# Recurrence gates of a two-block transformer: sigmoid in fp32 replaced by tanh of half the argument in three fp32r passes

## The chip, the cores and the metric

One core of one Trainium2 chip runs the whole program. The metric is the device time of one execution in microseconds (us). The engines that matter here are PE (TensorE: matrix products), DVE (VectorE) and ACT (ScalarE, which evaluates functions such as tanh, exp and the square root from a table that has to be loaded first). Each engine works through its own queue in order and waits at an instruction until what that instruction needs is there.

## The reference, cut to what matters

The reference runs two transformer blocks on 512 tokens of width 1024 in float32. The first block has a token mixer and a mixture of experts and is not touched. The second block prepends 16 meta tokens (528 rows), projects them, and combines for each of 8 heads an attention output with a recurrence over the tokens. The change lies in that recurrence, which runs once forward and once backward over each block of 128 channels:

```python
def rg_lru(xc, wa, ba, wx, bx, lam, reverse):
    ...
    r = jax.nn.sigmoid(jnp.einsum('btnc,ncd->btnd', xb, wa) + ba)
    i = jax.nn.sigmoid(jnp.einsum('btnc,ncd->btnd', xb, wx) + bx)
    log_a = RG_C * r * jax.nn.log_sigmoid(lam)
    a = jnp.exp(log_a)
    u = jnp.sqrt(-jnp.expm1(2.0 * log_a)) * (i * xf)
    _, h = lax.associative_scan(_linear_recurrence_combine, (a, u), axis=1, reverse=reverse)
```

Here `xc` is the projected input after a convolution over four tokens, `xb` the same in blocks of 128 channels, `xf` the same in float32. The output of both directions is multiplied by a gelu branch and a sigmoid gate and added to the gated attention output.

## The kernel before, in words

A matrix product that has to be nearly exact in float32 is done in three passes: both operands are split into a high part in fp32r (ACT copies it, `Net.split`, whose ACT copy is recorded at L90 and whose DVE subtraction at L170) and the low rest, and `mm3` (L196 to L200) multiplies high by high, high by low and low by high. `by_turns` reads the moving operand in two alternating halves, and `unturned` or an equivalent rearrangement puts the columns back where PSUM is read.

The stretch that the change touches is the loop in `block2` over the 8 heads n, called rounds here. PE's order is written out by hand. One round issues on PE, in this order: a projection of 24 matmuls of 512 columns (`gates`, first step), the product of the attention weights of head n-1 with the values (`attention`, L198 to L200 into psB), the gate products of the recurrence of head n (`rnn_gates`, L2046), two blocks of attention scores of head n (L198 to L200 into psD, 12 matmuls of 264 columns), the second projection, transposes of the normalized scores (L2140 with 16 rows, L2145 with 128), the third projection, two more blocks of scores, the recurrence's input projection for head n+1 (`rnn_x`, 48 matmuls of 264 columns) and again transposes. DVE and ACT are ordered by a planner which takes instructions in the order of the program as far as it expects them to be ready, so their order is not to be read from the source. Functions that need a table keep the program's order among themselves (`Net.act`).

`rnn_gates` makes four groups of products, two directions times the two gates r and i. Each group is two fp32 matmuls of 264 columns, which are recorded as two each, and fills one PSUM tile of the tag psD. There are two such tiles, shared with the attention scores and the 16-row transposes. ACT reads a group into `rg` or `ig` with a sigmoid (L90, rg<-psD and ig<-psD). They are named rg1, ig1, rg2 and ig2 below, in program order. DVE then multiplies ig by the convolved input (L2049).

In the round after, `rnn` (L2078) takes rg of head n-1: ACT makes a tanh and an exp of it and the square of that, DVE combines them (L2092). Later in the round ACT takes the two square roots, and DVE multiplies (L2098), scans (L2101), adds both directions (L2103) and multiplies by the gelu branch (L2104). The output of `attention` of head n-2 is completed behind this: an addition on DVE (L2163, ao), a split into `ga` by ACT (L90, ga<-ao) and `rn` by DVE. `rnn_x` makes the convolution in four DVE instructions (L2026, L2028).

ACT's table is loaded by an ACT_TABLE_LOAD which the compiler puts ahead of an activation that needs another one. A round has three: for the sigmoid, for the exp of the attention scores, for the square roots. Tanh needs none beside exp or sigmoid. Behind the loop the output projection follows (`mix_out`), with one square root for each of four token tiles and a gain `n2g` that a DMA brings.

Of the kernel before, what the change touches and what calls it, by code (L numbers as in the profile page):

```python
# [9 lines left out]
FT = mybir.dt.float32  # L10
FR = mybir.dt.float32r
I32 = mybir.dt.int32
BF = mybir.dt.bfloat16
AF = mybir.ActivationFunctionType
OP = mybir.AluOpType
# [38 lines left out]
def halves(x):  # L54

    return x.rearrange("p (s c) -> p s c", s=2)


def by_turns(x):

    return x.rearrange("p (s c) -> p c s", s=2)


def unturned(x):

    return x.rearrange("p (c s) -> p s c", s=2)
# [9 lines left out]
class Net:  # L76
# [1912 lines left out]
    def rnn_start(self, p, vec):  # L1989

        nc = self.nc
        x = vec[:, 72:88]
        cl = p.tile([128, 2, 16], FT, name="cl")
        y = p.tile([128, 16], FT, name="cl_y")
        c = cl[:, 0, :]
        nc.vector.scalar_tensor_tensor(y, x, -1.0, x, op0=OP.mult, op1=OP.min)
        self.act(y, y, AF.Exp)
        self.log1p_unit(p, c, y, 16)
        nc.vector.tensor_scalar(y, x, 0.0, None, op0=OP.min)
        nc.vector.tensor_tensor(c, y, c, OP.subtract)  # L2000
        nc.vector.tensor_scalar(c, c, 8.0, None, op0=OP.mult)
        nc.vector.tensor_scalar(cl[:, 1, :], c, -1.0, None, op0=OP.mult)
        return cl

    def rnn_x(self, p, n, vec, xT):

        nc, I = self.nc, self.I
        T = META + S
        H = T // 2
        nhi, nlo = xT  # L2010
        wg = p.tile([128, 2, 2, 128], FT, name="wg")
        nc.sync.dma_start(wg[:, 0], I["rg_wa_2"][0, :, n].rearrange("d c e -> c d e"))
        nc.sync.dma_start(wg[:, 1], I["rg_wx_2"][0, :, n].rearrange("d c e -> c d e"))
        hi, lo = self.wchunk(I["w_in_2"][0], 0, NK, 1536 + n * 128, 128)
        xr = p.tile([128, T + 3], FT, name="xr")
        nc.vector.memset(xr[:, 0:2], 0.0)
        nc.vector.memset(xr[:, T + 2:], 0.0)
        for j in range(2):
            js = slice(j * H, (j + 1) * H)
            ps = self.psA.tile([128, 512], FT, name="psA")  # L2020
            for k in range(NK):
                self.mm3(ps[:, :H], hi[:, k, :], lo[:, k, :], by_turns(nhi[:, k, js]), by_turns(nlo[:, k, js]),
                         k == 0, k == NK - 1)
            self.act(halves(xr[:, 2 + j * H:2 + (j + 1) * H]), unturned(ps[:, :H]), AF.Copy)
        c = p.tile([128, T], FT, name="xc")
        nc.vector.tensor_scalar(c, xr[:, 0:T], vec[:, n:n + 1], vec[:, 32 + n:33 + n], op0=OP.mult, op1=OP.add)  # L2026
        for j in range(1, 4):
            nc.vector.scalar_tensor_tensor(c, xr[:, j:j + T], vec[:, 8 * j + n:8 * j + n + 1], c,  # L2028
                                           op0=OP.mult, op1=OP.add)
        return c, wg  # L2030

    def rnn_gates(self, p, n, vec, x, meanwhile=lambda: None):

        nc = self.nc
        T = META + S
        H = T // 2
        c, wg = x
        rg = p.tile([128, 2, T], FT, name="rg")
        ig = p.tile([128, 2, T], FT, name="ig")
        for d in range(2):  # L2040
            if d:
                meanwhile()
            for w, dst, bias in ((0, rg, 40), (1, ig, 56)):
                ps = self.psD.tile([128, 2, 512], FT, name="psD")
                for j in range(2):
                    nc.tensor.matmul(ps[:, j, :H], wg[:, w, d, :], c[:, j * H:(j + 1) * H], start=True, stop=True)  # L2046
                self.act(dst[:, d, :].rearrange("p (a b) -> p a b", a=2), ps[:, :, :H], AF.Sigmoid,
                         bias=vec[:, bias + 8 * d + n:bias + 8 * d + n + 1])
        nc.vector.tensor_tensor(ig, ig, c[:, None, :].to_broadcast([128, 2, T]), OP.mult)  # L2049
        return rg, ig  # L2050

    def gates(self, p, n, xT, rn, ga):
# [25 lines left out]
    def rnn(self, p, n, cl, st, rn):  # L2078

        nc = self.nc  # L2080
        T = META + S
        rg, ig = st
        u = p.tile([128, 2, T], FT, name="th", bufs=1)
        for d in range(2):
            q = 8 * d + n
            r, t = rg[:, d, :], u[:, d, :]
            self.act(t, r, AF.Tanh, scale=cl[:, 1, q:q + 1])
            self.act(r, r, AF.Exp, scale=cl[:, 0, q:q + 1])

            a2 = p.tile([128, T], FT, name="a2", bufs=1)  # L2090
            self.act(a2, r, AF.Square)
            nc.vector.scalar_tensor_tensor(t, a2, 1.0, t, op0=OP.add, op1=OP.mult)  # L2092
        yield
        for d in range(2):
            self.act(u[:, d, :], u[:, d, :], AF.Sqrt, scale=0.0625)
        for d in range(2):
            t, g, r = u[:, d, :], ig[:, d, :], rg[:, d, :]
            nc.vector.tensor_tensor(g, g, t, OP.mult)  # L2098
            if d:
                t, g, r = t[:, ::-1], g[:, ::-1], r[:, ::-1]  # L2100
            nc.vector.tensor_tensor_scan(t, r, g, 0.0, op0=OP.mult, op1=OP.add)  # L2101
        f = u[:, 0, META:]
        nc.vector.tensor_tensor(f, f, u[:, 1, META:], OP.add)  # L2103
        nc.vector.tensor_tensor(rn[n], rn[n], f, OP.mult)  # L2104
        yield
# [227 lines left out]
```

## Time and profile before

| | us |
|---|---|
| median of 3 runs | 1918.06 (1916.91 to 1920.73) |
| the profiled execution | 1921.64 |
| its span, first to last instruction | 1919.8 |
| PE busy in the span | 1805.8 |
| DVE busy in the span | 990.5 |
| ACT busy in the span | 709.1 |

The profiled execution's own time is 1.84 us longer than its span. The loop over the heads lies between about 1244 and 1536 us of the span, a round of it takes 34.7 us. The recorded duration of a matmul includes its latency and overlaps with the next, so what a matmul costs is read from the distance between two starts.

### The profile page before, as it was taken

The numbers are of one execution on the slowest core, as the hardware profiler recorded it, in microseconds if no ns is written. First come the engines' busy times: TensorE is split into PE (matmuls) and PEld (weight loads), VectorE is DVE, ScalarE is ACT, GpSimd is POOL, SyncE is SP. The second block draws the span as 40 slices with busy tenths as digits, with TensorE's granted clock in tenths as the row PEclk, the third lists the DMA queues.
The fourth block names the chain that finished last, engine by engine and source line by source line (L and its number), as shares of the span: only waits on it lengthen the run. The fifth ranks groups of instructions, "written<-read, shape, count | busy, mean of one in ns | idle before, by whom it ended". The sixth has DMA issues, their size and how long they took to land.

```text
span 1919.8 us, 23894 instructions
## 1 busy us (share of the span) xinstructions
PE 1805.8 (94%) x9309; PEld 1365.1 (71%) x9309; DVE 990.5 (52%) x1834; ACT 709.1 (37%) x1157; POOL 30.5 (2%) x39
## 2 busy tenths in 40 slices
PE   6999999989999899989898879999999989999999
PEld 5787888868898734434333336888888778888887
DVE  6853787745466523222121249657878863333332
ACT  5243443424323311101010126467677733322322
POOL 0000000000000000000000000000000000000000
PEclk9999999989999899999999999999999999999999
DMA  8645766876288699999999973432221233333331
GB/s 257 96 119 99 123 93 87 148 180 88 72 292 308 241 372 425 424 426 425 424 425 425 383 301 121 122 104 78 72 76 56 88 99 110 99 100 107 101 121 66
DMA packets 251988, 372.13 MB, mean 194 GB/s; under 512 B 30369, under 2 KB 192706, under 8 KB 227938
## 3 DMA queue, kind: packets, MB, share of 16 engines
q1 hardware_dynamic: 241218, 342.79, 56.3%
q10 hardware_dynamic: 7632, 16.78, 2.3%
q0 software_dynamic: 3024, 11.01, 1.5%
q8 instruction: 74, 1.21, 0.3%
q14 instruction: 40, 0.33, 0.0%
HBM read 348.51 MB, written 22.04 MB: 193 GB/s over the span
## 4 chain that ended last, share of the span: by engine, by line
PE 56%; DMA 21%; DVE 14%; ACT 7%; issue 3%; SPq 0%; POOL 0%; ACTq 0%; DVEq 0%
DMA mwt<-in_w 16%; PE psA L199 13%; PE psA L200 12%; PE psA L198 12%; PE psB L1289 4%; DVE wlo L170 2%; PE psB L1322 2%; DMA raw<-in_w_in 2%; ACT whi L90 1%; DVE th L2101 1%; PE psA L1108 1%; PE psB L603 1%; PE psB L649 1%; DVE yc L594 1%; ACT th L90 1%
## 5 line engine op out<-in xcount | busy, mean ns | idle before, releaser
L90 ACT ACTIVATE whi<-raw 128x1024 fp32r<-128x1024 f32 (+1 forms) x203 | 233.4, 1156 | 418.1 <-PE psA L199 267.6
L170 DVE TENSOR_TENSOR wlo<-raw,whi 128x1024 fp32r<-128x1024 f32 (+1 forms) x195 | 249.8, 1283 | 242.7 <-ACT whi L90 230.3
L1289 PE MATMUL psB<-mwt,XT 128*64 128x512 f32 x1008 | 236.3, 602 | 12.7 <-DMA mwt<-in_w 9.9
L1289 PEld LDWEIGHTS psB<-mwt,XT 128*64 128x64 f32 x1008 | 79.3, 138 | 157.5 <-issue 131.3
L200 PE MATMUL psA<-hT_hi,wlo 128*128 128x512 f32 (+1 forms) x456 | 176.2, 386 | 9.2 <-DVE wlo L170 9.2
L199 PE MATMUL psA<-hT_lo,whi 128*128 128x512 f32 (+1 forms) x456 | 177.3, 389 | 0.0
L198 PE MATMUL psA<-hT_hi,whi 128*128 128x512 f32 (+1 forms) x456 | 175.9, 386 | 0.9 <-ACT whi L90 0.9
L1354 DVE TENSOR_TENSOR res<-res,psA 128x512 f32<-128x512 f32 x128 | 79.4, 682 | 126.3 <-PE psA L1349 126.3
L1322 PE MATMUL psB<-mwt,hbT 128*64 128x512 f32 x480 | 118.6, 596 | 22.6 <-DMA mwt<-in_w 21.3
L199 PE MATMUL psA<-hn_lo,whi 128*128 128x512 f32 (+1 forms) x368 | 136.4, 371 | 0.3 <-DVE hn_lo L2197 0.3
L198 PE MATMUL psA<-hn_hi,whi 128*128 128x512 f32 (+1 forms) x368 | 136.5, 371 | 0.2 <-ACT hn_hi L90 0.2
L200 PE MATMUL psA<-hn_hi,wlo 128*128 128x512 f32 (+1 forms) x368 | 136.3, 370 | 0.0
L1298 DVE TENSOR_TENSOR sl<-sl,psB 128x512 f32<-128x512 f32 x16 | 11.0, 688 | 193.7 <-PE psB L1289 193.7
L198 PE MATMUL psA<-xn_hi,whi 128*128 128x512 f32 (+1 forms) x320 | 109.4, 342 | 0.4 <-ACT qx L90 0.4
L200 PE MATMUL psA<-xn_hi,wlo 128*128 128x512 f32 (+1 forms) x320 | 108.2, 338 | 0.0
L199 PE MATMUL psA<-xn_lo,whi 128*128 128x512 f32 (+1 forms) x320 | 108.1, 338 | 0.0
L1322 PEld LDWEIGHTS psB<-mwt,hbT 128*64 128x64 f32 x480 | 36.3, 136 | 98.5 <-issue 57.2
L200 PEld LDWEIGHTS psA<-hT_hi,wlo 128*128 128x128 f32 (+1 forms) x456 | 86.1, 189 | 21.8 <-DVE wlo L170 10.2
L198 PEld LDWEIGHTS psA<-hT_hi,whi 128*128 128x128 f32 (+1 forms) x456 | 86.1, 189 | 13.6 <-ACT whi L90 1.3
L90 ACT ACTIVATE XT<-psA 128x512 f32<-128x512 f32 x32 | 17.5, 594 | 211.6 <-PE psA L1266 206.2
L199 PEld LDWEIGHTS psA<-hT_lo,whi 128*128 128x128 f32 (+1 forms) x456 | 86.1, 189 | 11.9
L198 PEld LDWEIGHTS psA<-hn_hi,whi 128*128 128x128 f32 x368 | 69.6, 189 | 9.5 <-ACT hn_hi L90 0.5
(571 smaller groups left out, 3489.8 us busy)
## 6 DMA issues: line engine op xcount, KB each, us to landing
mwt<-in_w SPq DMA_DIRECT2D x188, 1024.0 KB, 20.7
raw<-in_w_in SPq DMA_DIRECT2D x108, 512.0 KB, 7.2
raw<-in_w_ffn_in SPq DMA_DIRECT2D x44, 512.0 KB, 3.9
raw<-in_w_ffn_out SPq DMA_DIRECT2D x22, 512.0 KB, 3.6
raw<-in_w_pa SPq DMA_DIRECT2D x8, 512.0 KB, 4.3
raw<-in_w_pb SPq DMA_DIRECT2D x8, 512.0 KB, 5.1
raw<-in_w_o SPq DMA_DIRECT2D x8, 512.0 KB, 4.5
raw<-in_w_out SPq DMA_DIRECT2D x8, 512.0 KB, 3.6
```

The lines of the kernel that those rows point to most:

```text
L90: ins = self.nc.scalar.activation(out, in_, func, **kw)
L170: return self.nc.vector.tensor_tensor(lo, x, hi.bitcast(FT), OP.subtract)
L198: nc.tensor.matmul(out, whi, xhi, start=first, stop=False)
L199: nc.tensor.matmul(out, whi, xlo, start=False, stop=False)
L200: nc.tensor.matmul(out, wlo, xhi, start=False, stop=last)
L594: conv = nc.vector.scalar_tensor_tensor(yc, xc[:, j:j + S], self.cw[:, 24 * j + m:24 * j + m + 1], yc, op0=OP.mult, op1=OP.add)
L603: nc.tensor.matmul(psn[:, n, m:m + 1], sq[:, n * 128:(n + 1) * 128], one, start=True, stop=True)
L649: nc.tensor.matmul(ps[:, j, :, :], qk[:, h, 0, tok], qk[:, h, :, tok], start=True, stop=True)
L1108: nc.tensor.matmul(ps[:, k, :], self.res[:, t, :].rearrange("p (f k) -> p k f", k=NK)[:, k0 + k, :], P0[:, t, :], start=(t == 0), stop=(t ...
L1289: nc.tensor.matmul(ps[CAP * i:CAP * (i + 1), :], XT[:, r0 + k, CAP * i:CAP * (i + 1)], w_, start=(r0 + k == 0), stop=(r0 + k == NK - 1))
L1322: nc.tensor.matmul(pys[half][CAP * i:CAP * (i + 1), :], hT[:, r0 + k, CAP * i:CAP * (i + 1)], ws[i][:, k, half * 512:(half + 1) * 512], st ...
L1354: nc.vector.tensor_tensor(x, x, unturned(ps), OP.add)
```

## The change

The weights of the gate products and the convolved input are split into a high and a low part and the products go through `mm3`, three fp32r passes in place of one fp32 product. The sigmoid becomes a tanh of half the argument, and what follows is adapted: sigmoid(x) is (1 + tanh(x/2))/2, so the bias and the decay constants are halved ahead of the loop, ig gets its 1 added in the DVE multiplication, and the constants of tanh, exp and square root take up the rest. Behind the two square roots a tanh of one column into a scrap tile is added. The convolved input, the high part of the weights and the low part of the input have one buffer each, the high part of the input shares the two buffers of `xr`, and the low part of the weights those of `wg`.

```diff
@@ -1998,7 +1998,9 @@
         self.log1p_unit(p, c, y, 16)
         nc.vector.tensor_scalar(y, x, 0.0, None, op0=OP.min)
         nc.vector.tensor_tensor(c, y, c, OP.subtract)
-        nc.vector.tensor_scalar(c, c, 8.0, None, op0=OP.mult)
+        nc.vector.tensor_scalar(c, c, 4.0, None, op0=OP.mult)
+
+        nc.vector.tensor_scalar(vec[:, 40:72], vec[:, 40:72], 0.5, None, op0=OP.mult)
         nc.vector.tensor_scalar(cl[:, 1, :], c, -1.0, None, op0=OP.mult)
         return cl
 
@@ -2011,6 +2013,8 @@
         wg = p.tile([128, 2, 2, 128], FT, name="wg")
         nc.sync.dma_start(wg[:, 0], I["rg_wa_2"][0, :, n].rearrange("d c e -> c d e"))
         nc.sync.dma_start(wg[:, 1], I["rg_wx_2"][0, :, n].rearrange("d c e -> c d e"))
+        ws = p.tile([128, 2, 2, 128], FR, name="wghi", bufs=1), p.tile([128, 2, 2, 128], FR, name="wg")
+        self.split(*ws, wg)
         hi, lo = self.wchunk(I["w_in_2"][0], 0, NK, 1536 + n * 128, 128)
         xr = p.tile([128, T + 3], FT, name="xr")
         nc.vector.memset(xr[:, 0:2], 0.0)
@@ -2022,19 +2026,21 @@
                 self.mm3(ps[:, :H], hi[:, k, :], lo[:, k, :], by_turns(nhi[:, k, js]), by_turns(nlo[:, k, js]),
                          k == 0, k == NK - 1)
             self.act(halves(xr[:, 2 + j * H:2 + (j + 1) * H]), unturned(ps[:, :H]), AF.Copy)
-        c = p.tile([128, T], FT, name="xc")
+        c = p.tile([128, T], FT, name="xc", bufs=1)
         nc.vector.tensor_scalar(c, xr[:, 0:T], vec[:, n:n + 1], vec[:, 32 + n:33 + n], op0=OP.mult, op1=OP.add)
         for j in range(1, 4):
             nc.vector.scalar_tensor_tensor(c, xr[:, j:j + T], vec[:, 8 * j + n:8 * j + n + 1], c,
                                            op0=OP.mult, op1=OP.add)
-        return c, wg
+        cs = p.tile([128, T + 3], FR, name="xr")[:, 0:T], p.tile([128, T], FR, name="xclo", bufs=1)
+        self.split(*cs, c)
+        return c, cs, ws
 
     def rnn_gates(self, p, n, vec, x, meanwhile=lambda: None):
 
         nc = self.nc
         T = META + S
         H = T // 2
-        c, wg = x
+        c, (chi, clo), (whi, wlo) = x
         rg = p.tile([128, 2, T], FT, name="rg")
         ig = p.tile([128, 2, T], FT, name="ig")
         for d in range(2):
@@ -2043,10 +2049,13 @@
             for w, dst, bias in ((0, rg, 40), (1, ig, 56)):
                 ps = self.psD.tile([128, 2, 512], FT, name="psD")
                 for j in range(2):
-                    nc.tensor.matmul(ps[:, j, :H], wg[:, w, d, :], c[:, j * H:(j + 1) * H], start=True, stop=True)
-                self.act(dst[:, d, :].rearrange("p (a b) -> p a b", a=2), ps[:, :, :H], AF.Sigmoid,
+                    js = slice(j * H, (j + 1) * H)
+                    self.mm3(ps[:, j, :H], whi[:, w, d, :], wlo[:, w, d, :], by_turns(chi[:, js]), by_turns(clo[:, js]),
+                             True, True)
+                self.act(dst[:, d, :].rearrange("p (a s c) -> p a s c", a=2, s=2),
+                         ps[:, :, :H].rearrange("p a (c s) -> p a s c", s=2), AF.Tanh, scale=0.5,
                          bias=vec[:, bias + 8 * d + n:bias + 8 * d + n + 1])
-        nc.vector.tensor_tensor(ig, ig, c[:, None, :].to_broadcast([128, 2, T]), OP.mult)
+        nc.vector.scalar_tensor_tensor(ig, ig, 1.0, c[:, None, :].to_broadcast([128, 2, T]), op0=OP.add, op1=OP.mult)
         return rg, ig
 
     def gates(self, p, n, xT, rn, ga):
@@ -2084,15 +2093,17 @@
         for d in range(2):
             q = 8 * d + n
             r, t = rg[:, d, :], u[:, d, :]
-            self.act(t, r, AF.Tanh, scale=cl[:, 1, q:q + 1])
-            self.act(r, r, AF.Exp, scale=cl[:, 0, q:q + 1])
+            self.act(t, r, AF.Tanh, scale=cl[:, 1, q:q + 1], bias=cl[:, 1, q:q + 1])
+            self.act(r, r, AF.Exp, scale=cl[:, 0, q:q + 1], bias=cl[:, 0, q:q + 1])
 
             a2 = p.tile([128, T], FT, name="a2", bufs=1)
             self.act(a2, r, AF.Square)
             nc.vector.scalar_tensor_tensor(t, a2, 1.0, t, op0=OP.add, op1=OP.mult)
         yield
         for d in range(2):
-            self.act(u[:, d, :], u[:, d, :], AF.Sqrt, scale=0.0625)
+            self.act(u[:, d, :], u[:, d, :], AF.Sqrt, scale=0.25 ** 3)
+
+        self.act(self.small.tile([128, 1], FT, name="warm"), cl[:, 0, 0:1], AF.Tanh)
         for d in range(2):
             t, g, r = u[:, d, :], ig[:, d, :], rg[:, d, :]
             nc.vector.tensor_tensor(g, g, t, OP.mult)
```

## Rows read from the trace of the kernel before

**Rows 1.** The page's part 1: engine, busy us, share, instructions.
```profile
PE 1805.8 (94%) x9309; PEld 1365.1 (71%) x9309; DVE 990.5 (52%) x1834; ACT 709.1 (37%) x1157; POOL 30.5 (2%) x39
```
**Rows 2.** One round as a window: length, each engine's busy us, granted clock, DMA.
```profile
1353.38:1388.07 34.69, 33.62 (x196) 29.16 (x195) 27.77 (x53) 25.53 (x45) 0.00 (x0) 1.00 0.26 77
```
**Rows 3.** PE in order of time, round 2: start us, duration us, instruction [idle before].
```profile
1318.77 3.89 PE L2046 MATMUL psD<-xc,wg 128*128 128x264 f32 x16
1323.54 0.38 PE L198 MATMUL psD<-kThi,qhi 128*128 128x264 f32 x1 [0.88 <-ACT rg L90]
...
1324.99 0.38 PE L198 MATMUL psA<-xn_hi,whi 128*128 128x512 f32 x1
...
1330.17 0.67 PE L2140 MATMUL psD<-ident,pr 128*16 128x128 f32 x2
...
1343.48 0.38 PE L2140 MATMUL psD<-ident,pr 128*16 128x128 f32 x2
...
1353.38 3.89 PE L2046 MATMUL psD<-xc,wg 128*128 128x264 f32 x16
```
**Rows 4.** PE in order of time, a run of fp32r passes: first and 34th.
```profile
1303.47 0.28 PE L198 MATMUL psA<-xn_hi,whi 128*128 128x264 f32 x1
...
1307.18 0.28 PE L198 MATMUL psA<-xn_hi,whi 128*128 128x264 f32 x1
```
**Rows 5.** ACT in order of time, round 2, around the gates.
```profile
1319.86 0.70 ACT L90 ACTIVATE rg<-psD,vec 128x528 f32<-128x528 f32 x1 [0.92 <-PE psD L2046]
...
1322.27 0.63 ACT L90 ACTIVATE ga<-ao 128x512 fp32r<-128x512 f32 x1 [0.81 <-DVE xr L2017]
1322.80 0.68 ACT L90 ACTIVATE rg<-psD,vec 128x528 f32<-128x528 f32 x1
...
1326.75 1.28 ACT L90 ACT_TABLE_LOAD   x1 [2.18 <-DVE m L2127]
1328.04 0.80 ACT L90 ACTIVATE pr<-psD,m,qs 128x528 f32<-128x528 f32 x1
```
**Rows 6.** DVE in order of time, round 2 into round 3.
```profile
1337.70 0.70 DVE L2126 TENSOR_REDUCE m<-psD 128x1 f32<-128x528 f32 x1
...
1344.54 1.33 DVE L2098 TENSOR_TENSOR ig<-ig,th 128x528 f32<-128x528 f32 x2 [0.27 <-ACT th L90]
...
1348.61 0.75 DVE L2028 SCALAR_TENSOR_TENSOR xc<-xr,vec,xc 128x528 f32<-128x528 f32 x1
...
1356.25 0.67 DVE L2163 TENSOR_TENSOR ao<-ao,rn 128x512 f32<-128x512 f32 x1
```
**Rows 7.** Groups by line and form, 1235 to 1560: count, busy us, mean ns, idle.
```profile
L90 ACT ACT_TABLE_LOAD x25 | 32.1, 1283 | 29.9 <-DVE m L2127 17.5 <-DVE th L2101 9.3 <-DVE rn L2104 3.0
...
L90 ACT ACTIVATE pr<-psD,m,qs 128x528 f32<-128x528 f32 x32 | 25.2, 789 | 4.3 <-DVE m L2127 4.2
...
L170 DVE TENSOR_TENSOR qlo<-qf,qhi 128x512 fp32r<-128x512 f32 x8 | 5.4, 677 | 1.8 <-ACT qhi L90 1.8
...
L90 ACT ACTIVATE qhi<-qf 128x512 fp32r<-128x512 f32 x8 | 5.0, 628 | 0.0
```
**Rows 8.** Who waited for whom, 1235 to 1560: us in total, times, longest.
```profile
PE psD L198 <- ACT rg L90: 5.4, 6, 1.0
...
PE psD L198 <- DVE PTlo L170: 3.0, 2, 1.8
```
**Rows 9.** Behind the last round: ACT, PE, DVE in order of time, then a window.
```profile
1528.51 1.28 ACT L90 ACT_TABLE_LOAD   x1 [2.96 <-DVE rn L2104]
1529.81 0.74 ACT L90 ACTIVATE th<-rg,cl 128x528 f32<-128x528 f32 x1
...
1544.99 0.48 PE L198 MATMUL psD<-whi,ga 128*128 128x512 f32 x1 [2.01 <-ACT ga L90]
...
1556.48 1.28 DVE L2209 SCALAR_TENSOR_TENSOR hn_tok<-hB,mo_r,n2g 128x1024 f32<-128x1024 f32 x1 [1.08 <-DMA n2g<-in_norm_g]
...
1545.00:1549.00 4.00, 4.00 (x11) 3.26 (x12) 1.89 (x2) 2.00 (x2) 0.00 (x0) 0.59 0.95 262
```

## The prediction

> **What bounds the kernel now.** I read the page's first part, which says PE [rows 1], then windows of one round, because the mean over the program hides the stage. In a round of 34.69 us PE is busy for 33.6, DVE for 27.8 and ACT for 25.5, at the full clock [rows 2]. So PE's order sets the pace of the loop, and DVE has about 7 us to spare. PE in order of time shows the two places where PE itself loses time in each of rounds 2 to 6. Scores wait 0.88 us for ACT to empty a psD tile, and a pair of small transposes takes 0.67 us where the undisturbed pair takes 0.38 [rows 3]. Both waits lead to ACT: the first to rg2, which stands behind the split of ao and so behind DVE's 0.81 us [rows 5], the second to scores whose exp waited behind a table load of 1.28 us [rows 5]. From the first gate product to the next projection PE spends 1324.99 - 1318.77 = 6.22 us, of which 3.89 are gate products [rows 3].
>
> **Gate products.** Sixteen records in 3.89 us are 0.243 each, so an fp32 product of 264 columns (two records) costs 0.486 us. Three fp32r passes cost 0.337, since 33 distances between starts make 3.71 us, 0.1124 each [rows 4]. Eight products a round: 3.89 becomes 2.70, and 1.19 us of PE work goes in each of 8 rounds, 9.5 us in all. These rows are of the same shape, reading by turns, with weights changed at each pass.
>
> **The psD handover.** Faster products meet the two psD tiles sooner. ACT starts rg1 0.12 us after the group's work (1318.77 + 4 x 0.243 = 1319.74, then 1319.86), takes 0.70, and PE follows 0.06 after the end (1322.80 + 0.68 = 1323.48, then 1323.54) [rows 3, 5]. With 0.675 a group, counted from the first product: PE ends group 2 at 1.35, ACT frees the first tile at 1.50, group 3 runs from 1.56, rg2 ends near 3.15, and the scores run from 3.2. Their 12 passes and two restarts of 0.1 put the next projection at about 4.7, if ACT takes rg2 and ig2 without anything in between. Without any handover it would be 18 + 18 = 36 passes, 4.05 us; I keep that as the other bound. So rounds 2 to 6 gain 6.22 - 4.7 = 1.5 us each, 7.6 in all. Rounds 0, 1 and 7 have no such wait or another one: there I count the 1.19 saved less a new wait of 0.4 to 0.7, and in round 7 also most of its wait of 0.7 (the six waits for rg sum to 5.4 [rows 8]): 0.5, 0.7 and 1.5. Together 10.3 us.
>
> **Table loads.** There are 25 now, three a round [rows 7]. The sigmoid's goes; the exp's moves from behind the wait for the score maxima to directly behind the roots. The first round needs one, the seven others two, the last roots one and the tanh behind them one, and the output projection's root a new one: 18. Seven fewer are 9.0 us of ACT, which is not PE's time. What counts is that exp starts 1.28 us earlier after its maximum. The transposes then find their scores, and 0.67 - 0.38 = 0.29 us goes in each round, 2.4 in all. In round 7 two blocks wait for PTlo, 3.0 us together [rows 8]; the first hangs on the same exp and I take 0.8 of its 1.2.
> A page of the Trainium skill, "ScalarE: Activation LUTs", section "What ACT_TABLE_LOAD costs", adds a drain of about 1.38 us to each load of 1.28. Here the exp follows 0.01 us after the load's end, so the trace shows no such drain; with it the seven loads would be 18.6 us of ACT.
>
> **New work on ACT and DVE.** Each round adds two ACT copies (0.63 each, as qhi), two DVE subtractions (0.68 each, as qlo) [rows 7], and a warming tanh of some 0.2 us. Second pointer operands in four activations cost at most 0.789 - 0.628 = 0.16 each by those rows, 0.6 us. ACT gains and loses about the same. DVE rises from 27.8 to 29.2 us in a round that shrinks to about 32.9: it fits, but not everywhere. From the maximum at 1337.70 to the completed ao at 1356.92 DVE has a single gap of 0.27 us [rows 6]. The split of the weights needs only a DMA and the end of the last gate products, so I place it in the gap in which DVE waits for exp, free of charge. The split of the input comes right behind the convolution, inside the closed stretch, and delays ao by 0.7 less some 0.15 that the earlier exp gives back. PE is not held by it: the convolution ends at 1349.4, one copy, one subtraction and at worst one scan of 1.2 in front end by 1352, and the gates start at 1353.38 [rows 3, 6]. If a second scan and a weight split also go ahead of it, PE waits about 0.5 us a round, 4 us in all. The halving of constants is one small DVE instruction far ahead of the loop; the DVE multiplication changes its form, not its size. Both I count at nothing.
>
> **The end.** At 1528.51 ACT waited for DVE and only then loaded exp's table [rows 9]. With the table there the chain to the last ao is 1.28 us shorter, and PE waits 2.01 us at its end. Against that, the new load ahead of the first root of the output projection is 1.28 us long, of which 1.08 lies beside the wait for n2g [rows 9], so 0.2 is lost if that DMA keeps its place and 1.28 if not. I take a net gain of 0.8. Behind PE's wait the granted clock is 0.59 for 4 us, the lower level for most of it [rows 9]; a shorter wait might save up to 1.5 us, which I leave to the range.
>
> **Sum.** 10.3 + 2.4 + 0.8 + 0.8 = 14.3 us off a span of 1919.8, whose execution took 1921.64. The median of the runs shown is 3.6 lower, so I take the difference off 1918.06 and forecast 1904. Between the bounds (no handover 4.5 more, the clock 1.5 more; a late input split 4 less, the root 1.1 less) this case reaches from 1898 to 1910.
>
> **Rivals.** First, ACT's planned order stays as it is, with the split of ao ahead of rg2. Then rounds 2 to 6 gain nothing from faster products: the next projection comes at ao + 2.76, as now, and each round changes by ao's delay less 0.29. With 0.55 of delay that is +0.3 a round, 1.3 together; the rest (about 1.3 in round 0 and 0.3 + 0.7 in round 1, 1.0 in round 7, 1.6 at the exp and the end) leaves a gain of 3.6: 1914.5. For it speaks that this is today's order in five rounds. Against it: rg2 becomes ready 0.6 us earlier and ao 0.55 later, and today rg2's products end at 1318.77 + 2.92 = 1321.69, already before the split of ao starts at 1322.27 [rows 5]. If the split goes between rg2 and ig2 instead, the gain per round is 0.2 + 0.29, near 1911.
> Second, slower: the same order, and DVE's closed stretch grows by more. The place is the convolution: the warm tanh with its load, 1.5 us, can stand ahead of the second copy to xr, which comes behind the roots today, and hold the convolution for 1.1; the weights' subtraction can fall into the stretch, 0.7. Then ao comes 0.7 + 0.7 + 1.1 - 0.15 = 2.35 later, five rounds lose 2.06 each, and with 3 us gained elsewhere the time is 1925. It decides for slower from about 2 us of ao's delay. With rg2 and ig2 ahead of the split the same delay costs little, as nobody on PE waits for ao.
> Third, the change does not do what it says with the tables: the warming tanh could bring sigmoid's table, and exp would load again behind its maximum. That leaves the PE work and the handover but not the exp: about 14.3 - 2.4 - 0.8 - 1 = 10, 1908 to 1909. Today's 25 loads are two in round 0, three in each of seven rounds and two behind the loop; so none is left for the exp that follows the tanh at 1529.81, whose load comes behind roots too [rows 7, 9]. That speaks against.
> The Trainium skill, "ScalarE activation tables: per-element evaluation and per-set limits", section "Table sets in the compiler and the runtime", says that the back end places loads by the greedy longest run, and by that rule the set that also serves the coming exps is loaded; the trace agrees at 1528.51 to 1529.81.
>
> **How the numbers follow.** Forecast 0.55; the split ahead of rg2 with a small delay, 0.18; between rg2 and ig2, 0.11; slower, 0.10; tables, 0.06. The range from 1897 to 1919 leaves out the slower case and little else. 0.2% is 3.8 us, about what a measurement can tell from no change: faster takes the forecast, the in-between and the table case, and a third of the first rival, whose centre lies just at that edge, 0.77; I give 0.03 of it to unknown collisions: 0.74. Same takes most of the first rival, 0.14; slower 0.12.
>
> **What would show it.** In the changed profile, 192 fp32r passes at 0.11 us for the gates; 18 table loads, none behind the score maxima; ACT's order rg1, ig1, rg2, ig2, then ga; rounds of about 32.9 us; next projection 4.7 us behind the first gate product. The forecast is wrong if ga still stands ahead of rg2, if PE waits at the gate products for the input's low part, or if the convolution waits for the warm tanh.

## The result and the profile after

| | before | after |
|---|---|---|
| median | 1919.93 (8 runs) | 1930.94 (8 runs, 1928.16 to 1934.38) |
| ratio to before | | 1.0053, 95% interval 1.0039 to 1.0067 |
| profiled execution, its span | 1921.64, 1919.8 | 1932.93, 1930.8 |
| rounds 0 to 6, from first gate product to first gate product | 35.72, 33.93, 34.61, 34.69, 34.69, 34.70, 31.06 | 35.73, 34.69, 35.40, 37.08, 34.70, 37.08, 32.29 |
| from the last such mark to the end of the span | 431.3 | 433.8 |

The change is slower by 11 us where 14 us faster was forecast. Of the 10.95 us between the spans the seven rounds hold 7.56 and the stretch behind them 2.5; the rest had grown ahead of the loop.

What the change does, it does. Here are groups of the changed kernel by line and form, over the loop and the output projection (1235 to 1560): count, busy us, mean ns, idle time ahead.

```profile
L90 ACT ACT_TABLE_LOAD x17 | 21.8, 1283 | 0.3
L198 PE MATMUL psD<-xr,wghi 128*128 128x264 f32 x64 | 18.9, 296 | 7.0 <-ACT rg L90 4.2 <-ACT xr L90 2.4
L170 DVE TENSOR_TENSOR xclo<-xc,xr 128x528 fp32r<-128x528 f32 x8 | 5.6, 695 | 0.7 <-ACT xr L90 0.6
L90 ACT ACTIVATE rg<-rg,cl 128x528 f32<-128x528 f32 x16 | 13.1, 820 | 0.3
L170 DVE TENSOR_TENSOR wg<-wg,wghi 128x512 fp32r<-128x512 f32 x8 | 5.5, 692 | 13.7 <-ACT wghi L90 13.7
L90 ACT ACTIVATE xr<-xc 128x528 fp32r<-128x528 f32 x8 | 5.1, 643 | 21.6 <-DVE xc L2032 21.6
```

The window holds 17 table loads in place of 25 [rows 7], and the eighteenth, which was forecast for the output projection's root, stands just behind it:

```profile
1565.54 1.28 ACT L90 ACT_TABLE_LOAD   x1
```

There are 64 times three passes, and the split instructions cost what was forecast. Rounds 2 to 4 as windows (length, busy us of PE, PEld, DVE, ACT and POOL, granted clock, DMA share and GB/s), and below them a stretch inside round 3 and one at the last gate products:

```profile
1320.45:1355.85 35.40, 33.26 (x205) 29.34 (x204) 28.59 (x54) 25.64 (x46) 0.00 (x0) 1.00 0.26 75
1355.85:1392.93 37.08, 34.93 (x205) 30.52 (x204) 30.26 (x56) 26.27 (x47) 0.00 (x0) 0.95 0.25 72
1392.93:1427.62 34.69, 33.24 (x204) 29.34 (x203) 26.89 (x52) 25.21 (x45) 0.00 (x0) 1.00 0.24 69
1388.30:1393.00 4.70, 4.70 (x14) 3.63 (x14) 4.70 (x7) 2.06 (x3) 0.00 (x0) 0.64 0.02 5
1497.00:1506.00 9.00, 8.24 (x26) 6.34 (x27) 5.25 (x7) 2.81 (x4) 0.00 (x0) 0.62 0.39 117
```

At the full clock the rounds are not shorter than before [rows 2], and two of them, with the stretch at the last gates, lose to the lower granted clock: at most 2 x 0.05 x 37.08 + 0.38 x 9.00 = 7.1 us, if PE had work all that time. The rounds themselves show less: round 3 is 1.68 longer than round 2, which has the same two waits of PE, and round 4, which lacks one of them, is 0.70 shorter than round 2, so a fall costs about 1.0 us over two rounds. Against [rows 3, 5, 6] stand ACT, DVE and PE of the changed kernel in order of time, from the roots to the scores of one round (start us, duration us, instruction, [idle before, what ended it]):

```profile
1343.63 1.28 ACT L90 ACT_TABLE_LOAD   x1
1344.92 1.18 ACT L90 ACTIVATE th<-th 128x528 f32<-128x528 f32 x2
1346.12 1.28 ACT L90 ACT_TABLE_LOAD   x1
1347.41 0.20 ACT L90 ACTIVATE warm<-cl 128x1 f32<-128x1 f32 x1
1347.52 0.37 ACT L90 ACTIVATE xr<-psA 128x264 f32<-128x264 f32 x1
...
1356.90 0.63 ACT L90 ACTIVATE ga<-ao 128x512 fp32r<-128x512 f32 x1 [2.57 <-DVE ao L2174]
1357.44 0.68 ACT L90 ACTIVATE rg<-psD,vec 128x528 f32<-128x528 f32 x1
```

```profile
1346.85 2.40 DVE L2112 TENSOR_TENSOR_SCAN th<-rg,ig 128x528 f32<-128x528 f32 x2
1349.16 0.53 DVE L2030 TENSOR_SCALAR xc<-xr,vec 128x528 f32<-128x528 f32 x1
...
1351.36 0.67 DVE L170 TENSOR_TENSOR PTlo<-psB,PThi 128x512 fp32r<-128x512 f32 x1
...
1353.84 0.69 DVE L170 TENSOR_TENSOR xclo<-xc,xr 128x528 fp32r<-128x528 f32 x1
...
1356.20 0.67 DVE L2174 TENSOR_TENSOR ao<-ao,rn 128x512 f32<-128x512 f32 x1
```

```profile
1352.09 0.48 PE L198 MATMUL psB<-PThi,v_hi 16*128 16x512 f32 x1 [1.05 <-DVE PTlo L170]
...
1355.85 0.28 PE L198 MATMUL psD<-xr,wghi 128*128 128x264 f32 x1
...
1358.18 0.38 PE L198 MATMUL psD<-xr,wghi 128*128 128x264 f32 x1 [0.82 <-ACT rg L90]
...
1361.80 0.38 PE L198 MATMUL psA<-xn_hi,whi 128*128 128x512 f32 x1
```

Read downwards: on ACT the warming tanh and its load stand between the roots and the second copy to xr, so the convolution cannot begin before 1347.89; on DVE both scans, from 1346.85 on, stand ahead of it, and DVE has no break there. So the PTlo that frees a psB tile ends at 1352.03, and PE waits 1.05 us for it, a wait that no steady round had before (the two at PTlo in [rows 8] are for another tile). The split of ao stands ahead of all four gate activations, and in rounds 2, 3 and 5 PE waits once more, 0.82, between the second and the third gate group. The next projection comes 1361.80 - 1355.85 = 5.95 us behind the first gate product, where 4.7 was forecast and 6.22 was measured before.

### The profile page after: what moved, and what is told of

Read it like the earlier page. It is cut to its first block, busy times and chain, and to the rows that moved or that the text cites. A ratio compares the mean times of both kernels' runs of the same rounds, so it can differ in the third digit from the quotient of the medians.

```text
span 1930.8 us, 24060 instructions
## 1 busy us (share of the span) xinstructions
PE 1811.1 (94%) x9373; PEld 1373.5 (71%) x9373; DVE 997.8 (52%) x1851; ACT 712.4 (37%) x1174; POOL 30.5 (2%) x39
## 4 chain that ended last, share of the span: by engine, by line
PE 56%; DMA 21%; DVE 14%; ACT 6%; issue 3%; SPq 0%; POOL 0%; ACTq 0%; DVEq 0%
DMA mwt<-in_w 16%; PE psA L199 12%; PE psA L200 12%; PE psA L198 12%; PE psB L1289 4%; DVE wlo L170 2%; PE psB L1322 2%; DMA raw<-in_w_in 2%; ACT whi L90 1%; DVE th L2112 1%; PE psA L1108 1%; PE psB L603 1%; DMA m_pa<-pa_d 1%; PE psB L649 1%; DVE yc L594 1%
```

## The experiments

In the expectations letters stand for theories. A lays the loss to what comes with the tanh (the warming tanh, the scans that went ahead), B to the three passes and their splits, C, in e4's expectation alone, to the split of ao ahead of the gates, D to ACT's order alone, E to some loop that is not PE's work. F, formed behind the eighth run, names that loop. An order is changed with `self.after(x, y)`, which lets x stand behind y on its engine; "split last" means the split of ao behind the last gate activation.

**Each half of the change by itself.** e1 takes the three passes and keeps sigmoid, without the warming tanh and with the constants of before; e2 keeps the fp32 products and their operands and takes the rest. The core of each against the changed kernel, e1 first:

```diff
                 self.act(dst[:, d, :].rearrange("p (a s c) -> p a s c", a=2, s=2),
-                         ps[:, :, :H].rearrange("p a (c s) -> p a s c", s=2), AF.Tanh, scale=0.5,
+                         ps[:, :, :H].rearrange("p a (c s) -> p a s c", s=2), AF.Sigmoid,
...
-        self.act(self.small.tile([128, 1], FT, name="warm"), cl[:, 0, 0:1], AF.Tanh)
```
```diff
-        self.split(*cs, c)
...
-                    self.mm3(ps[:, j, :H], whi[:, w, d, :], wlo[:, w, d, :], by_turns(chi[:, js]), by_turns(clo[:, js]),
-                             True, True)
+                    nc.tensor.matmul(ps[:, j, :H], wg[:, w, d, :], c[:, j * H:(j + 1) * H], start=True, stop=True)
```

> Only the three fp32r passes with their splits; sigmoid, its table loads and the constants stay as before, and there is no warming tanh. Theory A (the time is lost because the warming tanh and its table load hold back the second copy to xr, DVE then runs both scans ahead of the convolution and the PTlo subtractions, and PE waits at the product with the values and falls to the lower clock): this kernel has neither, so it is not slower than before; DVE takes convolution and PTlo ahead of the scans; the granted clock stays 1.00 through rounds 2 to 6; rounds of 34.2 to 34.9 us; time 1912 to 1921. Theory B (the extra copies and subtractions of the splits cost it, DVE being too full): this kernel keeps most of the loss, 6 us or more above before, and PE waits at the product with the values as in the changed kernel.

> Only tanh for sigmoid and the warming tanh behind the roots; the gate products stay one fp32 pass without splits. Theory A: the scans stand ahead of the convolution here too, so it loses as the changed kernel does, or more, since the gate products also keep their 1.19 us a round: rounds of 35.5 to 38 us, granted clock under 1 in some rounds, time 1926 to 1942. Theory B: there are no splits, so no loss: at or below before, 1912 to 1920.

Measured: e1 1930.27, ratio 1.0053 (1.0036 to 1.007), rounds 2 to 5 of 36.62, 35.58, 36.70, 36.99 at granted clocks of 0.95, 1.00, 0.95, 0.95. e2 1927.62, ratio 1.0033 (1.0018 to 1.0049), rounds 36.27, 35.22, 37.60, 34.90 at 0.96, 0.99, 0.95, 1.00. So each half alone loses, and neither A nor B by itself is the cause. PE of e1 in order of time, at the scores of two rounds, and below it ao on DVE in the second of them:

```profile
1360.42 0.38 PE L198 MATMUL psD<-kThi,qhi 128*128 128x264 f32 x1 [2.22 <-ACT rg L90]
...
1395.72 0.38 PE L198 MATMUL psD<-kThi,qhi 128*128 128x264 f32 x1 [2.21 <-ACT rg L90]
```
```profile
1393.74 0.67 DVE L2170 TENSOR_TENSOR ao<-ao,rn 128x512 f32<-128x512 f32 x1
```

The same two instructions in round 4 of the kernel before:

```profile
1392.92 0.38 PE L198 MATMUL psD<-kThi,qhi 128*128 128x264 f32 x1 [0.95 <-ACT rg L90]
```
```profile
1390.94 0.67 DVE L2163 TENSOR_TENSOR ao<-ao,rn 128x512 f32<-128x512 f32 x1
```

The wait for rg2, 0.95 in this round (0.88 in that of [rows 3]), has become 2.21. Of the 1.26 us more, 0.64 comes from the products: the gates end 3.25 us behind their first start at 1390.26, with a handover in them, in place of 3.89. The other 0.61 comes from ao, which is complete 4.15 us behind that start in place of 3.54, with the input's low part (xclo) now ahead of it on DVE, and rg2 waits for its split. That is the first rival's place: the shorter products gain nothing there, and the delay of ao costs in full.

**The tanh part's order.** e3 is the changed kernel without the warming tanh, e4 with both scans behind the convolution and PTlo. First e3, then e4:

```diff
-        self.act(self.small.tile([128, 1], FT, name="warm"), cl[:, 0, 0:1], AF.Tanh)
```
```diff
-            nc.vector.tensor_tensor_scan(t, r, g, 0.0, op0=OP.mult, op1=OP.add)
+            self.after(nc.vector.tensor_tensor_scan(t, r, g, 0.0, op0=OP.mult, op1=OP.add), self.conv_last, self.pt_lo)
```

> The changed kernel without the warming tanh, nothing else. The exp table is then loaded at the first gate activation. Theory A: of the two scans one still stands ahead of the convolution, so PTlo ends about 1.2 us sooner than in the changed kernel, PE's wait at the product with the values shrinks from 1.2 us to 0.3 or less, and the clock stays up: rounds of 34 to 35 us, 1912 to 1922. Theory B: the splits are all there, so it stays within 4 us of the changed kernel's 1931.

> The changed kernel with one order added: each scan behind the convolution's last instruction and the last PTlo subtraction on DVE. The warming tanh stays where it is. Theory A: conv and PTlo move 1.2 to 2.4 us ahead; what is left is the hold of the second copy to xr by 1.5 us, so PE waits 0.3 to 1.0 us at the product with the values and keeps its clock: rounds of 34 to 35.2 us, 1912 to 1923. Theory B: within 4 us of 1931. A third theory C (the split of ao ahead of the first gate activation is what costs): here it stands behind rg2, so C also expects a gain, but of no more than the 0.8 us a round that PE waits for rg, 4 us in all, with the clock falling as before: 1925 to 1928.

Measured: 1930.27 (1.0034 to 1.0067) and 1928.84 (1.0032 to 1.0065). The wait for PTlo is gone in both, and a wait of 1.96 and 2.05 us at the scores stands in its place, so the gain that A expected did not come. The planner orders ACT anew with each edit: ga stood between ig1 and rg2 in e3 and between rg2 and ig2 in e4.

**Split last**, in e1's kernel (e5), in the kernel before (e6), in the changed one (e7), and in the changed one with the roots, and so the warming tanh, behind the second copy of xr and PThi (e8). The first edit is in all four, the second in e8 alone:

```diff
         self.split(*mix[h], o)
+        self.after(self.split_hi, self.gate_last)
```
```diff
-            self.act(u[:, d, :], u[:, d, :], AF.Sqrt, scale=0.25 ** 3)
+            self.after(self.act(u[:, d, :], u[:, d, :], AF.Sqrt, scale=0.25 ** 3), self.xr_last, self.pt_hi)
```

> The three passes with sigmoid and without the warming tanh, and one order added on ACT: the split of ao into ga behind the last gate activation of the round. Theory D (ACT's queue is what costs: the split of ao stands ahead of gate activations, waits for DVE there, PE waits for a psD tile, and a long wait also brings the lower clock): PE's wait of 2.3 us ahead of the scores falls below 0.6, the granted clock is 1.00 in rounds 2 to 6, rounds take 32.9 to 33.7 us, time 1905 to 1914. Theory E (DVE itself is the bound once the splits are on it, and the wait at ao only shows that): the wait moves elsewhere, to exp's maxima or to the transposes, and rounds stay at 34.5 or more: 1919 to 1930.

> The kernel before with the same order alone: the split of ao behind the last gate activation. Theory D: its wait of 0.88 us ahead of the scores goes in rounds 2 to 6 and 0.7 in round 7, rounds of 33.6 to 33.9 us, 4 to 6 us faster than before: 1914 to 1917. Theory E: DVE has the same work as before, the next wait takes its place: within 2 us of before.

> The changed kernel with the same order alone; the scans still stand ahead of the convolution. Theory D: the wait of 0.82 us between the second and the third group of gate products goes, the wait of 1.05 us for PTlo ahead of the product with the values stays: rounds of 34.0 to 34.8 us where the clock is full; if the clock still falls in two of five rounds, 2 us more in each: 1919 to 1926. Theory E: rounds of 35 us or more, 1927 to 1931.

> The changed kernel with two orders added: the split of ao behind the last gate activation, and the square roots (with the warming tanh behind them) behind the second copy to xr and the copies to PThi on ACT, so that the convolution and PTlo come first on DVE. Theory D: neither wait is left, clock 1.00, rounds of 32.7 to 33.4 us, time 1902 to 1911. Theory E: rounds of 34.5 or more, 1919 to 1930.

Measured: e5 1921.30, ratio 1.000 (0.9988 to 1.0012), rounds 2 to 5 of 34.48; e6 1919.35, 0.9987 (0.9973 to 1.0001), 34.54; e7 1926.02, 1.0024 (1.0012 to 1.0037), 34.68 where the clock held, with the wait for PTlo; e8 1921.38, 1.0006 (0.9993 to 1.0019), 34.70. So the loss goes with the order, but not one order gains, and the kernels with and without the shorter products stand at the same 34.5 to 34.7. That is E's outcome in e5, e6 and e8; e7 lies at the edge between D and E. Each time another wait fills the round: in e5 and e6 transposes wait for pr, 0.8 and 0.5 us, whose load and exp wait for the score maxima, which stand on DVE behind the multiplication of ig and the low part of ao; in e8 ACT's rg1 waits for a scan, since rg has two buffers and the second scan of two rounds ago still reads this one, and PE for rg1. ACT of e6, ACT of e8 and PE of e8:

```profile
1396.43 1.28 ACT L90 ACT_TABLE_LOAD   x1 [2.26 <-DVE m L2127]
```
```profile
1385.21 0.70 ACT L90 ACTIVATE rg<-psD,vec 128x528 f32<-128x528 f32 x1 [3.96 <-DVE th L2112]
```
```profile
1385.96 0.38 PE L198 MATMUL psD<-xr,wghi 128*128 128x264 f32 x1 [1.46 <-ACT rg L90]
```

Theory F reads this as one closed path: PE from the scores to the last product for xr, with hardly a wait; ACT's copy; DVE without a break through convolution, PTlo, scans and ao; ACT's gate activations and the split; the psD tile; the scores of the next round. The projection ahead of the gates, the product with the values and the gate products lie on PE beside DVE's stretch, in front of the wait. Work there costs nothing, and taking it away gains nothing.

This comes close to what the traces of e8 and e12 show, where the roots stand behind the copies of xr. In the kernel before its first half runs otherwise. PE's last product for xr starts at 1343.37, and ACT's copy of it only at 1344.95, behind a table load and both roots:

```profile
1343.37 0.28 PE L200 MATMUL psA<-xn_hi,wlo 128*128 128x264 f32 x1
```
```profile
1344.95 0.37 ACT L90 ACTIVATE xr<-psA 128x264 f32<-128x264 f32 x1
```

The chain that the profile follows back through this round (start us, us, what) leaves PE in the second projection and passes through ACT's functions of `rnn`, the score maxima, the exp, that load and the roots before it comes to DVE's stretch:

```profile
1323.54 0.38 PE psD L198
...
1330.21 1.06 ACT whi L90
...
1342.57 1.28 ACT L90
1343.87 0.65 ACT th L90
...
1358.23 0.38 PE psD L198
```

Both forms share the second half, from the convolution through ao and rg2 to the scores, and the next three runs try it and the gate products ahead of it.

**The loop tried in the kernel before.** e9 adds one unread DVE subtraction behind the convolution, e14 two; e10 does one of the eight gate products twice. The first edit is e9's, in e14 it stands twice; the second is e10's:

```diff
+        nc.vector.tensor_tensor(p.tile([128, T], FT, name="xclo", bufs=1), xr[:, 0:T], c, OP.subtract)
         return c, wg
```
```diff
-                    nc.tensor.matmul(ps[:, j, :H], wg[:, w, d, :], c[:, j * H:(j + 1) * H], start=True, stop=True)
+                    for _ in range(2 if (w, d, j) == (1, 0, 0) else 1):
+                        nc.tensor.matmul(ps[:, j, :H], wg[:, w, d, :], c[:, j * H:(j + 1) * H], start=True, stop=True)
```

> The kernel before, with one more DVE instruction a round: a subtraction of the convolved input from its unconvolved columns into a scrap tile, 128x528, behind the fourth instruction of the convolution. Nobody reads it. Theory that a closed loop through DVE sets the round (F): DVE runs without a break from the convolution to the addition that completes ao, so ao and the gate activation behind it come 0.70 us later in each round (the price of xclo in the changed kernel), PE's wait ahead of the scores grows from 0.88 to about 1.5, rounds 2 to 6 take 35.3 to 35.4 in place of 34.69, and the time rises by 4 to 6 us, ratio 1.002 to 1.003; more if the granted clock falls in a round. Theory of the prediction (PE's order sets the round, DVE has 7 us a round to spare): rounds of 34.69, ratio 1.000.

> The kernel before, with one of the eight fp32 gate products of a round done twice (the first half of the first ig group), 0.49 us more PE work a round; order on ACT and DVE as before. Theory F: the work lies in front of PE's wait for rg2, which shrinks from 0.88 to about 0.4, and the rounds 2 to 6 stay at 34.6 to 34.7; ratio 1.000 to 1.0005 (rounds 0, 1 and 7 may pay 0.5 each). Theory that PE's order sets the round: 35.18 a round, the time +3.4 to +3.9 us, ratio 1.002.

> The kernel before with two of the unread subtractions behind the convolution in place of one. Theory F: another 0.62 a round, the wait ahead of the scores grows from 1.95 to about 2.6, rounds of 35.9 at the full clock, ratio 1.0035. If the length of PE's wait brings the half clock: in the run with gate products in three passes alone PE waited 2.3 to 2.5 and most rounds had a stretch at the lower clock, so here also, rounds of 36.5 to 38 and a ratio over 1.006. If it is something of the new instructions: 35.9 in each round and the full clock.

Measured: e9 1923.26, ratio 1.0017 (1.0005 to 1.0029); e10 1921.93, 1.0005 (0.9993 to 1.0018); e14 1928.63, 1.004 (1.0023 to 1.0056). The windows of one round of e9, e10 and e14, from first gate product to first gate product:

```profile
1387.81:1423.11 35.30, 33.61 (x196) 29.15 (x195) 28.38 (x53) 25.50 (x45) 0.00 (x0) 1.00 0.24 68
```
```profile
1389.79:1424.47 34.68, 34.06 (x199) 29.61 (x197) 27.77 (x52) 25.49 (x45) 0.00 (x0) 1.00 0.24 69
```
```profile
1392.58:1428.50 35.92, 33.71 (x196) 29.24 (x195) 29.00 (x54) 25.43 (x44) 0.00 (x0) 1.00 0.23 67
```

0.69 us of DVE work, on an engine that is idle for 7 us of the round [rows 2], lengthens it by 0.62, and a second such instruction by 0.62 again. That is all of it, since from its start to that of the next instruction it takes 0.61 (1419.61 to 1420.22 in e9). 0.49 us of PE work, on the engine that is busy for 97% of the round, lengthens it by nothing: PE's wait in rounds 3 to 6 falls from 0.95 to 0.50 and its busy time rises from 33.6 to 34.06. PE of e10, against the 0.95 above:

```profile
1394.63 0.38 PE L198 MATMUL psD<-kThi,qhi 128*128 128x264 f32 x1 [0.50 <-ACT rg L90]
```

In round 1, where PE has no such wait, it is the other way round: 33.93 us before, 33.94 in e9 and e14, 34.38 in e10.

This is what F expects of the rounds, and it refutes the ground on which the forecast stood; e9's time rose by 3.6 us, a little less than the 4 to 6 expected.

**The loop shortened.** e11 is e8 with rg in a tile for each direction; e12 adds the score maxima ahead of the multiplication of ig and of the low part of ao; e13 adds ig in two tiles, the copy of the gate weights behind the last gate activation, and the subtractions of two projection weights behind the second scan; e15 puts the kernel before, with none of the change, into e13's order. The edits of e11 (for ig alike in e13), e12 (where the multiplication of ig and ao's low part are kept in `self.later` until the maxima are issued) and e13, which stand in e15 too as far as they apply:

```diff
-        rg = p.tile([128, 2, T], FT, name="rg")
+        rg = [p.tile([128, T], FT, name="rg%d" % d) for d in range(2)]
```
```diff
+    def flush(self):
+        for f in self.later:
+            self.after(f(), self.m_last)
```
```diff
         self.split(*ws, wg)
+        if n:
+            self.after(self.split_hi, self.gate_last)
...
+        ps = self.dense_fm(w_in, 4608 + n * 128, real)
+        if n > 1:
+            self.after(self.split_lo, self.scan_last)
```

> The changed kernel with the split of ao behind the last gate activation and the roots behind the copies of xr and PThi (the order of the earlier run that came out level), and rg kept in one tile for each direction, so that the first gate activation waits for the first scan of two rounds ago and no more for the second. In that earlier run it waited 3.96 us for the second scan, and PE 1.74 us behind it. Expected by theory F: PE's 1.74 us falls to about 0.3, but the loop's other arc then ends last: DVE runs from the convolution to the score maxima for 15.2 us without a break, exp and the scaling of the weights take 3.9, the transposes and the PE work to the second copy of the next xr 14.4, the copy and what DVE has ahead of it 1.3, together 34.4 to 34.7. So rounds of 34.2 to 34.5, 1917 to 1921 us. If the wait for the second scan alone held the rounds: rounds of 33.2, 1911 us.

> The run with rg in two tiles, and on DVE the score maxima ahead of the multiplication of ig (1.25 us) and the low part of ao (0.70 us), which today stand ahead of them in the closed stretch from the convolution to the maxima. Theory F: this arc of the loop gets 1.9 us shorter, PE's own work (about 32.7 us a round) or a wait for scan two becomes the bound, rounds of 32.8 to 33.4, 1908 to 1913 us, faster than both kernels. If DVE's stretch is not the loop, rounds stay where they are in the run without this.

> The run with the maxima first, and three things more taken out of the way between the convolution and the scores: on DVE the subtractions of two projection weights (wlo, 1.22 us each) go behind the second scan in place of ahead of the convolution and ahead of that scan; on ACT the copy of the gate weights (wghi, 0.63) goes behind the last gate activation; ig too is kept in one tile for each direction, so that the first ig activation waits for the first scan only. Theory F (PE's work from the scores to the second copy of xr, then DVE's stretch from the convolution to the second scan, then ACT's gate activations back to the scores): the loop becomes over 1 us shorter and PE's own work, 34.00 less its waits of 0.17, 0.46 and 0.58, so about 32.8, takes over: rounds of 32.7 to 33.1, 1910 to 1914 us, ratio 0.995 to 0.997. If that stretch is not in the loop: 34.0 as before, 1918 us.

> The kernel before (fp32 gate products, sigmoid, no warming tanh), in the order of the run with the stretch shortened: split of ao behind the last gate activation, roots behind the copies of xr and PThi, rg and ig in a tile for each direction, score maxima ahead of the multiplication of ig and the low part of ao, both subtractions of projection weights behind the scans. If the order alone gives the gain, rounds as in that run, 32.9 to 33.0, and 1911 to 1913 us. If the change's terms are worth what the prediction said once the loop is out of the way: PE's gate products take 3.73 us from their first start to the next product in place of 3.36 there, +0.37, and the maxima's exp waits for its table load of 1.28 us, so that the transposes wait 0.3 to 1.3 us: rounds of 33.6 to 34.6, 1916 to 1920 us, ratio 0.998 to 1.0005.

Measured: e11 1917.82, ratio 0.9985 (0.9975 to 0.9995); e12 1919.03, 0.9988 (0.9976 to 1.0); e13 1912.09, 0.9954 (0.9938 to 0.997); e15 1914.66, 0.9959 (0.9945 to 0.9973). One round each of e11, e12, e13 and e15:

```profile
1389.03:1423.04 34.01, 32.96 (x204) 29.34 (x203) 28.83 (x54) 25.75 (x46) 0.00 (x0) 1.00 0.25 71
```
```profile
1388.07:1422.07 34.00, 32.96 (x204) 29.34 (x203) 28.58 (x54) 25.81 (x46) 0.00 (x0) 1.00 0.24 71
```
```profile
1385.64:1418.57 32.93, 32.70 (x205) 29.27 (x203) 28.26 (x55) 25.91 (x46) 0.00 (x0) 1.00 0.25 73
```
```profile
1384.58:1418.14 33.56, 33.56 (x196) 29.29 (x195) 27.76 (x53) 25.75 (x44) 0.00 (x0) 1.00 0.25 72
```

e11's rounds came out between the two expectations (its time within the first), and e12 missed: the maxima lie behind the scores, so in these orders they are not on the path that ends last. What held e11 and e12 stands in e12's PE, which waits for ig1 and for ig2, and on ACT, where ig1 waits for the second scan and ig2 stands behind the copy of the gate weights:

```profile
1391.05 0.38 PE L208 MATMUL psD<-xr,wghi 128*128 128x264 f32 x1 [0.40 <-ACT ig L90]
...
1393.18 0.38 PE L208 MATMUL psD<-kThi,qhi 128*128 128x264 f32 x1 [0.52 <-ACT ig L90]
```
```profile
1390.29 0.70 ACT L90 ACTIVATE ig<-psD,vec 128x528 f32<-128x528 f32 x1 [0.65 <-DVE th L2124]
...
1391.91 0.63 ACT L90 ACTIVATE wghi<-wg 128x512 fp32r<-128x512 f32 x1 [0.33 <-PE psD L209]
```

With those gone (e13) the round is 32.93 and PE waits for almost nothing: now PE's order does set the pace. What each of e13's edits is worth by itself was not tried. e15 shows that most of the gain belongs to the order: the kernel before gains 1.12 us a round by it, to a round in which PE is busy throughout, and the change adds 33.57 - 32.93 = 0.64 to that. All of the 0.64 lies between the first gate product and the next projection: 1390.04 - 1384.58 = 5.46 in e15, 1390.46 - 1385.64 = 4.82 in e13. The times of e13 and e15, 1912.09 and 1914.66, have overlapping intervals; that the change itself gains is seen in the rounds, not in the times. Both beat the kernel before.

## Why the prediction was wrong

- **What bounds the kernel.** The step that failed. [Rows 2] give PE 33.62 of 34.69 us, and the prediction took from it that PE's order sets the pace and that DVE has 7 us to spare. DVE's spare time lies where nobody needs it; between the convolution and ao it has none [rows 6], and that stretch lies on a closed path with PE's wait for rg2 [rows 3]. e9, e10 and e14 show it: 0.62 us a round for each DVE instruction of 0.69, nothing for 0.49 us on PE. The prediction had read both rows, and the 0.88 us of PE's wait were the sign: an engine that waits in each round at the same place does not set the round.
- **Gate products, 9.5 us.** The passes cost 0.337 a product as forecast, and the saving was 0 in the order of before (e1: PE left the gates 0.64 earlier and waited 1.26 longer). Where PE is the bound, the scores start 3.36 us behind the first gate product (1385.64 to 1389.00 in e13), where 3.2 was forecast, in place of 3.79 (e15).
- **Handover, next projection 4.7 us behind the first gate product.** 5.95 in the changed kernel, for the split of ao stood ahead of all four gates; 4.82 in e13, where it stood behind them. Of the 6.22 - 4.7 = 1.52 forecast for a round 0.88 was PE's wait, which e15's order removes without the change; the other 0.64 is what e13 has over e15. So the mechanism and the size were right, and the order assumed, and with it PE as the bound, was not there. That order was asked of the time of rg2 and ao alone, and the planner, which orders by its own estimates, put the split further ahead, not further back.
- **Tables.** 18 loads, none behind the maxima, as forecast, and the transposes lost their 0.29. In the changed kernel no round got shorter by it. The load that moved up, with the warming tanh 1.4 us (1346.12 to 1347.52), stood ahead of the second copy of xr. The Trainium skill's page "ScalarE: Activation LUTs", section "What ACT_TABLE_LOAD costs", adds a drain of about 1.38 us to each load; the changed kernel's rows again show none, as the second load starts 0.02 us behind the roots and the tanh 0.01 behind the load.
- **New work.** "It fits" was wrong for xclo: 0.70 us inside the stretch, whose delay of ao was counted as costing PE nothing, and e9 shows that such work costs 0.62 a round. Durations were right: xclo 695 ns, the weights' subtraction 692, the copies 643 and 621; the second pointer operand 820 - 727 = 93 ns where at most 160 was allowed.
- **The end, 0.8 us.** From the last first gate product on the changed kernel took 433.8 in place of 431.3, with the 9 us at the lower clock in it, so the term cannot be read there. In e8 that stretch took 430.4. No run tried the term by itself.
- **Rivals.** The second named the place (the warming tanh ahead of the second copy of xr) and the sign, at 1925 and a chance of 0.10. It put the price on ao; what came was a wait for PTlo, the split ahead of all gates, and the lower clock, and that made 1931. Its place alone is not the cause: e3, without the warming tanh, lost as much. The first (products shorter, wait longer) is what e1 shows. Both rest on ao holding PE, which is the closed path, and together they had less than a third of the chances.

What brought the lower clock, which by the bound above makes up to 7 of the 11 us, is not settled. It came in kernels with longer waits of PE (and in round 0 of e5 and e13), but e3 waited 1.97 us in one round and fell to a mean of 0.95, and 1.96 in the next and kept 1.00, and e14, with waits of 0.30 and 1.78 a round, kept 1.00 throughout.

## What to carry to other kernels

A busy share of 97% does not make an engine the bound of a loop: if it waits at the same place in every round, follow that wait backwards until the path closes on itself a round earlier, and count as gain only what is taken out of that path. A cheap test is to add a little work to each suspected engine: the round grows by that much only on the path. The chain that the profile follows back is a first place to look: in the kernel before it left PE for most of the round. Where a planner orders the queues, a change in any duration can move an instruction past another, so the order of the changed kernel has to be counted among the unknowns; and buffers close such paths as well as data do (rg1 behind a scan of two rounds ago).

## What the runs showed of the hardware

The granted clock fell to a mean of 0.64 over 4.70 us in rounds 3 and 5 of the changed kernel, the lower of its two levels for most of that time, and stayed at 1.00 in rounds 2 and 4, so that the same work with the same two waits took 37.08 us in round 3 and 35.40 in round 2. Ahead of the fall in round 3 PE had been busy for 1.25 us of 2.30 (1386.00 to 1388.30), with its wait of 1.04 for PTlo in them; the same wait stood at the end of rounds 2 and 4, and the clock stayed at 1.00 there. A pointer as the bias of an activation, beside one as its scale, costs 93 ns at 528 columns (727 before, 820 after); the Trainium skill states the same 93 ns in the section named above. The warming tanh of a single column takes 0.20 us, but it brings its load of 1.28 to the place where it stands.
